# A hybrid RG-LRU and gated-delta-rule block: the order of all instructions planned anew, with a clock in the planner and a table of shifts to its priorities

## The chip, the cores and the metric

The kernel runs on one core of a Trainium2 chip. The core has a matrix engine (TensorE, PE in the profile; its weight loads are the row PEld), a vector engine (VectorE, DVE), a scalar engine (ScalarE, ACT), GpSimd (POOL) and a sync engine (SyncE, SP), which here issues every DMA. Each engine works through its own instructions in the order in which the program holds them; semaphores hold an instruction back until what it needs is there. The metric is the device time of one execution in microseconds (us): the median of the runs shown.

## The reference, cut to what matters

One layer on 1024 tokens of width 1024, all in float32:

```python
mod = silu(c) @ w_mod + b_mod                     # six vectors: sh1, sc1, g1, sh2, sc2, g2
h = rms_norm(x, norm_mix_w) * (1 + sc1) + sh1
proj = h @ w_in                                   # (1024, 3080): x_lru, y_lru, q, k, v, z, beta, alpha
xr = causal_conv(x_lru) + bias                    # RG-LRU half: two gates, a scan over the tokens,
out_lru = rms_norm(rg_lru(xr, ...) * gelu(y_lru)) # times gelu(y)
q, k, v = silu(causal_conv(q, k, v))              # gated delta rule half: 4 heads of 128
o = gated_delta_rule_chunked(q, k, v, g, beta)    # per chunk a triangular solve, then a recurrence
out_gdn = rms_norm(o) * silu(z)
x = x + g1 * (concat(out_lru, out_gdn) @ w_out)
h = rms_norm(x, norm_mlp_w) * (1 + sc2) + sh2
x = x + g2 * (square(relu(h @ w_up)) @ w_down)    # width 4096
out = rms_norm(x, final_norm_w)
```

## The kernel before

Nothing is issued where it is written. The body calls proxies (`PE`, `V`, `A`, `G`, `SP` for the five engines), and `Recorder.add` stores each call as an `Op` with an estimated duration (`Proxy.length`) and its dependencies. At the end `schedule` simulates the engines with these durations and picks one order for each engine; `emit` issues in that order. All instructions therefore carry one source line, that of the helper (L328 before the change, L427 after it), and the profile is read by names of tiles.

What sets the order: the big products form the *backbone* (`bb`): the projections in the sequence k0, k1, k2, k3, z0 to z3, q0, v0, q1, v1 and so on, then lx and ly (the two RG-LRU inputs), `wg` and `wl` (the output projection, GDN and LRU half), the MLP `up` and `dn`. They run in that fixed sequence. Everything else is side work: it has a latest start `lst`, from which a priority `pri` is made, and side work that is ready goes ahead of the backbone. The backbone is thus the filler in which side work on TensorE (token transposes, small products) finds its place.

Names that the steps below need. A projection is done in thirds of 342 tokens, `k0_p2`, `k0_p0`, `k0_p1`, 24 matmuls each (three products of a high and a low half of the operands: `hh`, `hl` and `_wh`, `_wl`). `sh1_c` turns the summed shift vector `sh1_acc` into columns; the third that ends the tokens needs it, as does `ab2`, the last third of beta and alpha. For head h, `key` makes `k{h}T` (a convolution of four VectorE or ScalarE steps, then a silu whose tanh is `k{h}th`), its transposes `ktok{h}`, the Gram products `kk{h}`, norms `ssk`, `rnk`, coefficients `bcoef`, the decay matrix `k{h}_dm` (GpSimd adds a mask `neg` to the broadcast `k{h}_gb`, ScalarE takes exp, GpSimd multiplies by `bcoef`) and the chunk matrix `LT`. `inverse` needs all four heads: a forward substitution of 31 steps on VectorE (`ftmp`, `xx`), transposes `xnc` and `xtc`, 16 copies into `xn` on ScalarE, and four rounds of small products on TensorE, `ie`, `ig`, `ih`, `ix`. `chain` is the recurrence over 8 chunks for each head: `ch` (three products a step), `r` and the state `S` on VectorE, `vn` on ScalarE, `cho` the output. `gate` are the gate products of RG-LRU, from `xrh` and `xrl`. `h2T` are the transposes ahead of the MLP. `z_wl`, `q_wl`, `v_wl` are low halves of weights, made by GpSimd.

Of the kernel before, what the change touches and what calls it, by code (L numbers as in the profile page):

```python
# [3 lines left out]

# [7 lines left out]
F32R = mybir.dt.float32r  # L12
AF = mybir.ActivationFunctionType
# [26 lines left out]
LAT = {("PE", "DVE"): 0.2, ("PE", "ACT"): 0.2, ("ACT", "DVE"): 0.04, ("DVE", "ACT"): 0.04, ("ACT", "POOL"): 0.08,  # L40
       ("DVE", "POOL"): 0.08, ("POOL", "DVE"): 0.04, ("POOL", "ACT"): 0.04, ("DVE", "PE"): 0.06, ("ACT", "PE"): 0.06,
       ("POOL", "PE"): 0.06, ("DVE", "DVE"): 0.04, ("ACT", "ACT"): 0.04, ("POOL", "POOL"): 0.05, ("PE", "PE"): 0.0}
COLD = 11.0
SC1_SUM = 5
SIDE_SCALE = 1.4
TINY_RUN, TINY_SHARE = 0.2, 1.0
# [1 line left out]
LOAD_WINDOW, DUE = 40.0, 5.0  # L48
# [3 lines left out]
class Buf:  # L52


    def __init__(self, pool, tag, bufs, shape, dt, name, proto):
        self.pool, self.tag, self.bufs, self.shape, self.dt, self.name, self.proto = pool, tag, bufs, shape, dt, name, proto
        self.tile = None
        self.key = (id(pool), tag)
        self.left = 0
        self.last = 0.0  # L60
        self.held = False
        self.pri = 1e9

    def get(self):
        if self.tile is None:
# [52 lines left out]
    return ap.name, (0, 1, lo, lo + sum((n - 1) * st for st, n in ap.ap) + 1)  # L118


class Op:
    __slots__ = ("port", "eng", "fn", "a", "k", "outs", "ins", "dur", "bb", "preds", "succs", "allocs", "bufs", "lst", "ready",
                 "need", "load", "bias", "pri", "tiny")


class Recorder:
# [11 lines left out]
    def add(self, eng, fn, a, k, outs, ins, dur, port=False):  # L138
        op = Op()
        op.port = port  # L140
        op.eng, op.fn, op.a, op.k, op.dur, op.bb, op.load = eng, fn, a, k, dur, self.bb and eng == "PE", False
        op.bias = None if self.early else self.bias
        op.tiny = self.tiny
        op.preds, op.succs, op.allocs = {}, [], []
        i = len(self.ops)
        op.bufs = {}
        for is_out, aps in ((False, ins), (True, outs)):
            for ap in aps:
                key, box = ap.box() if isinstance(ap, View) else dram_box(ap)
# [12 lines left out]
        if op.bb:
# [12 lines left out]
    def schedule(self):  # L175
        ops = self.ops
# [5 lines left out]
        for i in range(len(ops) - 1, -1, -1):  # L182
            op = ops[i]
            t = op.lst if op.bb else t
            op.pri = i - 1e5 if op.bias is None else op.lst if op.bb else min(op.lst, t + DUE + op.bias) + 1e-6 * i
        order = []
        now = {e: 0.0 for e in ("PE", "DVE", "ACT", "POOL", "SP")}
        dma = tend = 0.0
# [21 lines left out]
        while done < len(ops):  # L210
# [21 lines left out]
            i = heapq.heappop(avail[e])[1]  # L232
            if e == "PE" and debt > TINY_RUN:

                j = next((j for j in avail[e] if ops[j[1]].bb), None)
                if j:
                    avail[e].remove(j)
                    heapq.heapify(avail[e])
                    heapq.heappush(avail[e], (cls(ops[i]), i))
                    i = j[1]  # L240
            op = ops[i]
            t = now[e]
            wait = None
            while bbn < len(bbq) and ops[bbq[bbn]].ready is None:
                bbn += 1
            ref = ops[bbq[bbn]].lst if bbn < len(bbq) else 0.0
            op.allocs = [b for b in op.bufs if b.held != "in"]
            for b in op.allocs:
                f = free[b.key]
                q = queue[b.key]  # L250
                while q and q[0].held == "in":
                    q.pop(0)
                keep = 0
                lim = RESERVE.get(b.tag, 0)
                for o in q:
                    if o.pri >= op.pri or keep >= lim and (o.pri > -5e4 or o.tag != "b"):
                        break
                    if o.held != "in" and o is not b:
                        keep += 1
                if (op.load or not op.preds) and op.pri - ref > LOAD_WINDOW:  # L260
                    wait = ("t", t + 1.0)
                elif len(f) <= keep:
                    wait = ("b", b.key)
                elif f[0][0] > t + 1e-6:
                    wait = ("t", f[0][0])
                if wait:
                    break
# [11 lines left out]
            if e == "SP":  # L279
                now[e] = t + 0.05  # L280
                dma = max(dma, t + 1.25) + op.dur
                fin = dma
            else:
                t = max(t, port) if op.port else t
                now[e] = fin = t + op.dur * (2 if e == "PE" and t < COLD else 1)
                port = max(port, fin) if op.port else port
            op.ready = None
            order.append(i)
            done += 1
            for b in op.bufs:  # L290
                b.left -= 1
                b.last = max(b.last, fin)
# [38 lines left out]
def free_size(ap):  # L331
    n = 1
    for d in ap.shape[1:]:
        n *= d
    return n


class Proxy:
# [26 lines left out]

    def length(self, name, out, ins, k):
        n = max([free_size(out)] + [free_size(v) for v in ins[:1]])
        ptr = sum(free_size(v) == 1 for v in ins[1:]) and n > 1
# [7 lines left out]
        if self.eng == "DVE":  # L376
# [1204 lines left out]
```

## Time and profile before

| | |
|---|---|
| median of 3 runs | 1186.23 us (1186.09 to 1186.87) |
| the profiled execution | 1185.62 us, of which 1183.8 us lie between its first and last instruction (the span) |
| busy in the span | PE 1145.0, PEld 984.2, DVE 828.9, ACT 616.8, POOL 373.5 us |
| mean granted TensorE clock | 0.989 |
| 16 DMA engines | 55.9% busy with the kernel's own queue, 229.52 MB moved |

The profile is one execution. A row of its timeline gives the start (us from the first instruction), the length, the engine, the operation with its output and inputs, how many were merged, and in brackets how long the engine stood idle before and what released it. A busy engine is not always an engine at full rate: PE rows overlap, since matmuls are pipelined. The clock of TensorE falls to half in some stretches; the views by window give its mean.

### The profile page before, as it was taken

How to read it: one execution, taken by the hardware profiler on the slowest of the kernel's cores; microseconds unless marked ns; L12 is line 12 of the kernel's file. 1: busy time of each engine (PE TensorE's matmuls, PEld its weight loads, DVE VectorE, ACT ScalarE, POOL GpSimd, SP SyncE). 2: the span in 40 equal slices, each digit the busy share in tenths (PEclk: the TensorE clock that was granted, in tenths of full speed). 3: DMA queues.
4: the chain of work that ended last, by engine and by line, in shares of the span. 5: the costliest groups of instructions: out<-in, count | busy, mean ns of one | idle time of the engine just before them, and what ended most of it. 6: DMA issues, size and time to landing. Idle time of an engine off the chain costs nothing.

```text
span 1183.8 us, 15997 instructions
## 1 busy us (share of the span) xinstructions
PE 1145.0 (97%) x5952; PEld 984.2 (83%) x5952; DVE 828.9 (70%) x1123; ACT 616.8 (52%) x988; POOL 373.5 (32%) x221
## 2 busy tenths in 40 slices
PE   6799899999999999999999999999999999999997
PEld 3699899999999998877888888888788888888885
DVE  5757696578887798977966666756767556785553
ACT  5537327445455868277655555555555533353441
POOL 1319611345323472410011212121430075732130
PEclk9899899999999999999999999999999999999999
DMA  9703432533553525323077778776899767865631
GB/s 323 240 21 142 143 107 78 182 116 108 181 192 90 196 86 217 107 107 116 32 237 257 244 262 251 258 237 231 314 405 402 273 213 251 298 234 186 205 143 71
DMA packets 127151, 229.52 MB, mean 194 GB/s; under 512 B 10657, under 2 KB 51806, under 8 KB 127074
## 3 DMA queue, kind: packets, MB, share of 16 engines
q1 hardware_dynamic: 127074, 228.51, 55.9%
q8 instruction: 46, 0.75, 0.3%
q14 instruction: 31, 0.25, 0.1%
HBM read 171.83 MB, written 56.65 MB: 193 GB/s over the span
## 4 chain that ended last, share of the span: by engine, by line
PE 82%; DVE 8%; DMA 3%; ACT 3%; issue 2%; POOL 1%; SPq 1%; POOLq 0%; DVEq 0%; ACTq 0%
PE dn L328 26%; PE upx L328 15%; PE upz L328 8%; PE upy L328 4%; PE v_p L328 3%; PE q_p L328 3%; PE ly_p L328 3%; PE wg L328 3%; PE wl L328 3%; PE z_p L328 2%; PE k_p L328 2%; PE lx_p L328 2%; PE ch L328 2%; DVE xr L328 1%; SPq L328 1%
## 5 line engine op out<-in xcount | busy, mean ns | idle before, releaser
L328 PE MATMUL upx<-h2h,U 128*128 128x512 f32 x512 | 167.8, 394 | 0.0
L328 POOL TENSOR_TENSOR wd<-wd,wd 128x512 f32<-128x512 f32 x32 | 44.5, 1397 | 233.2 <-DMA wd<-in_w_down_dram 186.6
L328 PEld LDWEIGHTS upx<-h2h,U 128*128 128x128 f32 x512 | 96.1, 188 | 22.7
L328 PE MATMUL upx<-h2l,U 128*128 128x512 f32 x256 | 101.0, 395 | 0.0
L328 ACT ACTIVATE act<-act 128x512 f32<-128x512 f32 x112 | 70.9, 633 | 57.7 <-DVE act L328 55.5
L328 DVE TENSOR_TENSOR U<-wu,U 128x512 fp32r<-128x512 f32 x112 | 79.9, 733 | 18.0 <-ACT U L328 18.0
L328 PE MATMUL upz<-h2h,U 128*128 128x512 f32 x256 | 85.0, 394 | 0.0
L328 ACT CAST U<-wu 128x512 fp32r<-128x512 f32 x112 | 66.7, 617 | 14.1 <-PE upz L328 4.9
L328 DVE TENSOR_TENSOR act<-upz,ek 128x512 f32<-128x512 f32 x32 | 22.1, 691 | 56.5 <-PE upz L328 39.8
L328 PEld LDWEIGHTS upz<-h2h,U 128*128 128x128 f32 x256 | 48.1, 188 | 11.4
L328 PEld LDWEIGHTS upx<-h2l,U 128*128 128x128 f32 x256 | 48.1, 188 | 11.4
L328 ACT COPY ek<-upx 128x512 f32<-128x512 f32 x48 | 28.1, 585 | 48.2 <-PE upx L328 48.0
L328 PE MATMUL upz<-h2l,U 128*128 128x512 f32 x128 | 50.4, 394 | 0.0
L328 POOL TENSOR_TENSOR xb<-xb,keep 128x512 f32<-128x512 f32 x8 | 12.5, 1562 | 120.2 <-DVE keep L328 120.2
L328 PE MATMUL upy<-h2h,U 128*128 128x512 f32 x128 | 42.7, 394 | 0.0
L328 ACT ACTIVATE vn<-ch,bcoef 128x128 f32<-128x128 f32 x32 | 11.8, 368 | 53.0 <-PE ch L328 52.9
L328 POOL TENSOR_TENSOR ssq<-ssq,mhalf 128x1 f32<-128x1 f32 x16 | 11.3, 706 | 89.0 <-DVE ssq L328 88.9
L328 PE MATMUL k_p<-hl,k_wh 128*128 128x342 f32 x96 | 32.8, 341 | 0.3 <-DVE hl L328 0.3
L328 PE MATMUL k_p<-hh,k_wh 128*128 128x342 f32 x96 | 32.5, 339 | 0.4 <-ACT hh L328 0.4
L328 DVE TENSOR_TENSOR wu<-wu,wu 128x512 f32<-128x512 f32 x48 | 32.5, 682 | 0.2 <-DMA wu<-in_w_up_dram 0.2
L328 PE MATMUL k_p<-hh,k_wl 128*128 128x342 f32 x96 | 32.3, 336 | 0.0
L328 PE MATMUL v_p<-hh,v_wl 128*128 128x342 f32 x96 | 32.1, 335 | 0.0
(574 smaller groups left out, 3733.6 us busy)
## 6 DMA issues: line engine op xcount, KB each, us to landing
L<-aod SPq DMA_DIRECT2D x56, 512.0 KB, 7.0
R<-in_w_down_dram SPq DMA_DIRECT2D x40, 512.0 KB, 5.6
wu<-in_w_up_dram SPq DMA_DIRECT2D x32, 512.0 KB, 4.3
aod<-as SPq DMA_DIRECT2D x64, 256.0 KB, 2.4
wd<-in_w_down_dram SPq DMA_DIRECT2D x32, 512.0 KB, 4.8
aod<-act SPq DMA_DIRECT2D x48, 256.0 KB, 2.1
x<-in_x_dram SPq DMA_DIRECT2D x16, 512.0 KB, 4.8
sc_w<-in_w_mod_dram SPq DMA_DIRECT2D x16, 512.0 KB, 6.3
```

The lines of the kernel that those rows point to most:

```text
L328: op.fn(*[res(v) for v in op.a], **{n: res(v) for n, v in op.k.items()})
```

## The change

The planner is altered, and with it the order on every engine; what is computed, by which instructions and on which engine, stays as it was.

[...]
- A table `SHIFTS`, found by a search, holds one number for each of the 8378 recorded operations (2910 are not zero); a quarter of it, in us, is added to the priority of side work. Backbone operations and those recorded as `early` (the first loads and their use) take no shift.
- An accumulation that starts a PSUM tile anew must follow the one that ended in it; loads that are held back for being over 40 us ahead of the backbone are woken when the backbone has moved on, and no longer tried again each us; after small side work the backbone operation that comes next is the lowest in priority, and no longer the first found; durations with two column operands get two additions.

The core of the diff:

```diff
+_SHIFTS = (
+    'c-qaId2m(NeaC<AJ?ZI5LLdnV0RkZwiG4R<wm^)7YrMprIwncm)J@}Qn;B2s&a}-;-8P+MlCeAWA6YtW)=nmlGmY(z3C0fC21AT77@NiHn8ip4f%'
...
+SHIFTS = array.array("h", zlib.decompress(base64.b85decode(_SHIFTS))) if _SHIFTS else None
+class Clock:
+    def __init__(self):
+        self.end, self.work, self.over, self.half = HAM_0, 0.0, 0.0, True
+
+    def run(self, t, dur, work):
+        while t >= self.end:
+            share = self.work / HAM_W
+            self.half = share < HAM_UP if self.half else share < HAM_DOWN
+            self.end += HAM_W
+            self.work = min(self.over, HAM_W)
+            self.over -= self.work
+        if self.half:
+            dur, work = 2.0 * dur, 2.0 * work
+        now = min(work, self.end - t)
+        self.work += now
+        self.over = work - now
+        return dur
...
+        op.adj = SHIFTS[len(self.ops)] / 4.0 if SHIFTS else 0.0
+        op.work = min(dur, (1 if ins[-1].dtype == F32R else 2 if fn.__name__ == "transpose" else 4)
+                      * free_size(outs[0]) / 2400.0) if eng == "PE" else 0.0
...
-            op.pri = i - 1e5 if op.bias is None else op.lst if op.bb else min(op.lst, t + DUE + op.bias) + 1e-6 * i
+            op.pri = i - 1e5 if op.bias is None else op.lst if op.bb else min(op.lst, t + DUE + op.bias) + op.adj + 1e-6 * i
...
-                j = next((j for j in avail[e] if ops[j[1]].bb), None)
+                j = min((j for j in avail[e] if ops[j[1]].bb), default=None)
...
-                    wait = ("t", t + 1.0)
+                    wait = ("l", 0)
...
-                now[e] = fin = t + op.dur * (2 if e == "PE" and t < COLD else 1)
+                now[e] = fin = t + (clock.run(t, op.dur, op.work) if e == "PE" else op.dur)
...
-            return (0.145 if psum else 0.155) + n / (1920.0 if fast else 960.0) + (0.06 if ptr else 0.0)
+            return (0.145 if psum else 0.155) + n / (1920.0 if fast else 960.0) + 0.06 * ptr
```

Three places show what moved. The numbers behind the names only tell buffers apart.

GpSimd, where the decay matrices of the four key heads are made. Before:

```order
L328 TENSOR_TENSOR rnk_943<-ssk_921,mhalf_115 128x8
L328 TENSOR_TENSOR k0_dm_972<-k0_gb_905,neg_140 128x1024
L328 TENSOR_TENSOR k1_dm_1015<-k1_gb_908,neg_140 128x1024
L328 TENSOR_TENSOR k2_dm_1041<-k2_gb_929,neg_140 128x1024
L328 TENSOR_TENSOR k3_dm_1060<-k3_gb_974,neg_140 128x1024
L328 TENSOR_TENSOR k0_dm_972<-k0_dm_972,bcoef_987 128x1024
L328 MEMSET xt0_1083 128x1024
```

The same place on GpSimd after the change:

```order
L427 TENSOR_TENSOR k0_dm_935<-k0_gb_894,neg_120 128x1024
L427 TENSOR_TENSOR k1_dm_961<-k1_gb_896,neg_120 128x1024
L427 TENSOR_TENSOR k2_dm_1004<-k2_gb_963,neg_120 128x1024
L427 TENSOR_TENSOR k3_dm_1030<-k3_gb_968,neg_120 128x1024
L427 TENSOR_TENSOR rnk_1046<-ssk_937,mhalf_104 128x8
L427 MEMSET xn0_1060 128x1024
L427 TENSOR_TENSOR k0_dm_935<-k0_dm_935,bcoef_1063 128x1024
```

The norm of head 0 (`rnk`), which waits for VectorE, stood ahead of the four mask additions, and now stands behind them.

VectorE, about the convolution of the third key head, `k2T`. Before:

```order
L328 TENSOR_TENSOR LT_1085<-kk0_0_912,k0_dm_972 128x512
L328 TENSOR_TENSOR LT_1085<-kk0_1_923,k0_dm_972 128x512
L328 SCALAR_TENSOR_TENSOR k2T_984<-k2_st_366,cols_485,k2T_984 128x1024
L328 TENSOR_TENSOR bcoef_987<-beta_727,rnk_943 128x8
L328 SCALAR_TENSOR_TENSOR ncoef_1019<-ssk_921,rnk_943 128x8
L328 TENSOR_TENSOR bcoef_987<-bcoef_987,rnk_943 128x8
L328 SCALAR_TENSOR_TENSOR k2T_984<-k2_st_366,cols_485,k2T_984 128x1024
L328 COPY k3_b_1150<-k3_p2_948 128x1
L328 SCALAR_TENSOR_TENSOR k2T_984<-k2_st_366,cols_485,k2T_984 128x1024
L328 TENSOR_TENSOR LT_1085<-kk1_0_1005,k1_dm_1015 128x512
L328 TENSOR_TENSOR LT_1085<-kk1_1_1012,k1_dm_1015 128x512
L328 SCALAR_TENSOR_TENSOR k2T_984<-k2th_1187,k2T_984 128x1024
```

The same place on VectorE after the change; the first of the three steps of `k2T` stands seven instructions ahead of the first row here:

```order
L427 TENSOR_TENSOR bcoef_1063<-beta_735,rnk_1046 128x8
L427 SCALAR_TENSOR_TENSOR ncoef_1065<-ssk_937,rnk_1046 128x8
L427 TENSOR_TENSOR bcoef_1063<-bcoef_1063,rnk_1046 128x8
L427 SCALAR_TENSOR_TENSOR k2T_959<-k2_st_337,cols_475,k2T_959 128x1024
L427 COPY k3_b_1080<-k3_p2_951 128x1
L427 SCALAR_TENSOR_TENSOR k2T_959<-k2_st_337,cols_475,k2T_959 128x1024
L427 TENSOR_TENSOR LT_1114<-kk0_1_930,k0_dm_935 128x512
L427 TENSOR_TENSOR LT_1114<-kk0_0_918,k0_dm_935 128x512
L427 SCALAR_TENSOR_TENSOR k2T_959<-k2th_1116,k2T_959 128x1024
```

The convolution of `k2T` stood behind the `LT` rows of head 0 and its end behind those of head 1; now its three steps stand ahead of the former and its end ahead of the latter. On TensorE `ktok2` and `kk2`, which use it, stand 11 matmuls into `z0`, where they stood 54 matmuls into it; `ktok3` and `kk3` stand where they stood, two matmuls into `z1`.

TensorE, about the shift vector in the opening. Before:

```order
L328 MATMUL k1_p1_578<-hh3_300,k1_wh_423 128x342
L328 MATMUL k1_p1_578<-hl3_317,k1_wh_423 128x342
L328 MATMUL sh1_c_595<-ones_104,sh1_acc_445 128x1 x8
L328 MATMUL k1_p1_578<-hh3_300,k1_wl_436 128x342
L328 MATMUL k1_p1_578<-hh4_371,k1_wh_423 128x342
```

The same place on TensorE after the change:

```order
L427 MATMUL k1_p1_573<-hh7_388,k1_wh_427 128x342
L427 MATMUL k1_p1_573<-hl7_395,k1_wh_427 128x342
L427 MATMUL sh1_c_608<-ones_132,sh1_acc_409 128x1 x8
L427 MATMUL k1_p1_573<-hh7_388,k1_wl_442 128x342
L427 MATMUL ab2_639<-hh0_278,wab1_314 16x342
```

Twelve of the 13 matmuls of `k1_p1` that stood between `sh1_c` and `ab2` now stand ahead of `sh1_c`. Farther on, 14 matmuls of `v0_p2` stand ahead of the first `ie`, where 4 stood, and the first `ie` is that of head 3, behind six of the `xn` copies on ScalarE, where it was head 0's behind four; `gate20` and `gate2512` begin 10 matmuls into `ly3_p1`, where they began ahead of `ly3_p2`, 58 backbone matmuls earlier; the `h2T` of six of the eight token tiles stand 1 to 4 matmuls later, of one 8 earlier. The small vectors `alog` and `dtb` are loaded after `k3_w` and no longer ahead of `sh1_w`. On TensorE the order from the last `h2T` to the end is the same but for the place of four small products for `g2`; on the other engines it differs to nearly the end.

More of the change, by code (lines that the diff above doesn't have):

```diff
@@ L1 @@
+import array
+import base64
 import heapq
 import math
+import zlib
 from contextlib import ExitStack
@@ L42 @@
        ("POOL", "PE"): 0.06, ("DVE", "DVE"): 0.04, ("ACT", "ACT"): 0.04, ("POOL", "POOL"): 0.05, ("PE", "PE"): 0.0}
-COLD = 11.0
+HAM_W, HAM_0, HAM_DOWN, HAM_UP = 3.4133, 0.5, 0.5, 0.75
 SC1_SUM = 5
@@ L62, in __init__ @@
         self.pri = 1e9
+        self.sum = None
     def get(self):
@@ L121 @@
 class Op:
-    __slots__ = ("port", "eng", "fn", "a", "k", "outs", "ins", "dur", "bb", "preds", "succs", "allocs", "bufs", "lst", "ready",
+    __slots__ = ("adj", "work", "port", "eng", "fn", "a", "k", "outs", "ins", "dur", "bb", "preds", "succs", "allocs", "bufs", "lst", "ready",
                  "need", "load", "bias", "pri", "tiny")
@@ L161, in add @@
                 (ws if is_out else rs).append((box, i))
+        if eng == "PE" and fn.__name__ == "matmul":
+            b = outs[0].buf
+            if k["start"] and b.sum is not None:
+                op.preds.setdefault(b.sum, 0)
+            elif not k["start"] and k["stop"]:
+                b.sum = i
         if op.bb:
@@ L193, in schedule @@
         bbn = tmp = 0
+        ref, late = ops[bbq[0]].lst, []
         port = 0.0
+        clock = Clock()
         debt = 0.0
@@ L243, in schedule @@
             wait = None
-            while bbn < len(bbq) and ops[bbq[bbn]].ready is None:
-                bbn += 1
-            ref = ops[bbq[bbn]].lst if bbn < len(bbq) else 0.0
             op.allocs = [b for b in op.bufs if b.held != "in"]
@@ L270, in schedule @@
                     heapq.heappush(fut[e], (wait[1], i))
+                elif wait[0] == "l":
+                    heapq.heappush(late, (op.pri, i))
                 else:
@@ L289, in schedule @@
             done += 1
+            if op.bb:
+                bbn += 1
+                ref = ops[bbq[bbn]].lst if bbn < len(bbq) else 0.0
+                while late and late[0][0] - ref <= LOAD_WINDOW:
+                    j = heapq.heappop(late)[1]
+                    heapq.heappush(fut[ops[j].eng], (max(ops[j].ready, t), j))
             for b in op.bufs:
@@ L367, in length @@
         n = max([free_size(out)] + [free_size(v) for v in ins[:1]])
-        ptr = sum(free_size(v) == 1 for v in ins[1:]) and n > 1
+        ptr = sum(free_size(v) == 1 for v in ins[1:]) if n > 1 else 0
         psum = any(isinstance(v, View) and v.buf.tag == "ps" for v in ins)
@@ L381, in length @@
                 return 0.05 + n / 550.0
-            return (0.145 if psum else 0.155) + n / (1920.0 if fast else 960.0) + (0.06 if ptr else 0.0)
+            return (0.145 if psum else 0.155) + n / (1920.0 if fast else 960.0) + 0.06 * ptr
         if self.eng == "ACT":
-            return (0.16 if psum else 0.195) + n / 1200.0 + (0.1 if ptr or "accum_out" in k else 0.0)
+            return (0.16 if psum else 0.195) + n / 1200.0 + 0.1 * max(ptr, "accum_out" in k)
         if k.get("op") == ALU.pow:
```

49 lines of the change are left out of this document (added).

## The prediction

> **What bounds the kernel now.** First the page's head and its chain of work that ended last, then TensorE's idle time by stage.
>
> ```profile
> span 1183.8 us, 15997 instructions
> PE 82%; DVE 8%; DMA 3%; ACT 3%; issue 2%; POOL 1%; SPq 1%; POOLq 0%; DVEq 0%; ACTq 0%
> ```
>
> TensorE carries 82% of the chain. So the question is where it is not running. The next view gives the busy time of each engine in stretches that I cut at the stages (columns: stretch, its length, PE, PEld, DVE, ACT, POOL, granted clock, DMA share, GB/s).
>
> ```profile
> 0.00:60.00 60.00, 43.85 (x219) 30.04 (x220) 39.63 (x75) 31.80 (x49) 16.24 (x22) 0.91 0.82 278
> 60.00:113.00 53.00, 53.00 (x348) 50.98 (x348) 33.61 (x87) 30.50 (x75) 25.82 (x18) 0.97 0.20 81
> 113.00:135.00 22.00, 16.75 (x103) 16.21 (x102) 15.83 (x27) 10.38 (x19) 17.71 (x17) 0.84 0.46 161
> 172.00:210.00 38.00, 36.37 (x313) 36.02 (x312) 28.42 (x46) 25.73 (x50) 6.88 (x4) 1.00 0.28 89
> 210.00:310.00 100.00, 100.00 (x705) 99.47 (x705) 74.00 (x100) 46.78 (x81) 38.92 (x15) 1.00 0.46 151
> 310.00:345.00 35.00, 32.62 (x234) 31.68 (x233) 30.61 (x39) 16.68 (x29) 16.40 (x7) 1.00 0.35 108
> 345.00:400.00 55.00, 53.38 (x360) 51.53 (x358) 42.95 (x54) 35.96 (x53) 18.71 (x7) 1.00 0.44 142
> 400.00:500.00 100.00, 98.45 (x521) 87.48 (x520) 90.02 (x74) 61.27 (x78) 49.30 (x20) 1.00 0.44 158
> 500.00:557.00 57.00, 54.44 (x265) 43.62 (x263) 40.27 (x92) 39.46 (x83) 5.16 (x8) 1.00 0.32 111
> 557.00:1176.00 619.00, 619.00 (x2670) 500.21 (x2668) 400.74 (x465) 307.06 (x453) 168.56 (x99) 1.00 0.69 238
> 1176.00:1183.80 7.80, 0.17 (x1) 0.00 (x0) 2.29 (x4) 1.44 (x3) 0.55 (x1) 0.63 0.26 98
> ```
>
> Length less PE is what an order can win. From 557 to 1176 it is zero: 619 us that no order shortens. The opening idles 16.2 us under a DMA share of 0.82, the end 7.6 us behind the last matmul; both are mostly chains that the change leaves in place. What remains is 5.25 us at the key heads (113 to 135), 1.6 at the triangular inverse (172 to 210), and 2.4 + 1.6 + 1.55 + 2.6 = 8.1 us in recurrence, gates and second norm. Third view: what TensorE waited for there (us in total, times, longest).
>
> ```profile
> PE ktok L328 <- DVE k3T L328: 4.2, 1, 4.2
> PE sh_c L328 <- DVE hab L328: 2.1, 1, 2.1
> PE ch L328 <- DVE r L328: 1.7, 2, 1.3
> PE ie L328 <- ACT xn L328: 1.6, 1, 1.6
> PE gate L328 <- ACT xrh L328: 1.6, 2, 1.4
> PE ch L328 <- DVE S L328: 1.5, 2, 1.2
> PE h2T L328 <- DVE h2r L328: 1.5, 3, 0.5
> PE ktok L328 <- DVE k2T L328: 1.1, 1, 1.1
> ```
>
> Fourth, the clock, by windows of the trace's own stretches (same columns):
>
> ```profile
> 61.95:65.36 3.41, 3.41 (x14) 2.85 (x13) 1.54 (x15) 1.46 (x7) 1.88 (x1) 0.50 0.00 0
> 113.16:116.57 3.41, 2.33 (x21) 2.07 (x20) 3.23 (x5) 2.97 (x7) 3.27 (x6) 1.00 0.39 156
> 116.57:119.99 3.42, 3.42 (x26) 3.42 (x25) 3.42 (x7) 0.78 (x1) 2.80 (x3) 1.00 0.28 109
> 123.40:130.20 6.80, 5.53 (x26) 5.56 (x27) 5.06 (x8) 3.86 (x8) 4.68 (x7) 0.50 0.35 143
> ```
>
> After the wait for `k3T` TensorE ran 5.5 us at half clock, which costs 5.5 / 2 = 2.8 us more. After `sh_c` one stretch of 3.4 us cost 1.7.
>
> **The change part by part.** No instruction is added or removed, so each term is a wait that goes, comes or moves.
>
> *Opening.* Twelve matmuls now run ahead of `sh1_c`, and four more of `k1_p0` stand between `rows_ps` and it. A matmul of 342 columns lasts 26.29 / 166 = 0.158 us by this row of the chain:
>
> ```profile
> 130.02 26.29 PE z_p L328 x166
> ```
>
> Twelve are 1.9 us of work in a wait of 2.1 us. But `ab2` now follows `sh1_c` at once and must wait for `sh1`, which the 13 matmuls covered; I estimate 0.7 us for two small steps between (0.36 each, like `bcoef` below), and 0.6 us more idle ahead of `rows_ps`, whose cover loses the four matmuls (4 x 0.158). Gain 2.1 - 0.7 - 0.6 = 0.8 us; bounds 2.1 (the whole wait) and -1.3 (the wait stays, the new one comes). The SP queue loses two small loads ahead of `sh1_w`, worth at most their issue; taken as nothing, because the DMA engines are at 0.82.
>
> *Key heads.* GpSimd, VectorE and one row of TensorE, by the timeline (the last bracket is the idle time ahead of the row):
>
> ```profile
> 90.15 2.61 POOL L328 TENSOR_TENSOR rnk<-ssk,mhalf 128x8 f32<-128x8 f32 x1 [23.39 <-DVE ssk L328]
> 92.73 10.21 POOL L328 TENSOR_TENSOR k_dm<-k_gb,neg 128x1024 f32<-128x1024 f32 x4
> 104.83 1.29 DVE L328 TENSOR_TENSOR LT<-kk,k_dm 128x512 f32<-128x512 f32 x2 [4.15 <-POOL k_dm L328]
> 113.23 1.21 DVE L328 SCALAR_TENSOR_TENSOR k2T<-k2th,k2T 128x1024 f32<-128x1024 f32 x1
> 114.50 1.09 PE L328 MATMUL ktok<-ident,k2T 128*128 128x128 f32 x8 [1.07 <-DVE k2T L328]
> 122.00 2.52 DVE L328 SCALAR_TENSOR_TENSOR k3T<-k3th,k3T 128x1024 f32<-128x1024 f32 x1 [0.54 <-ACT k3th L328]
> 133.73 0.36 DVE L328 TENSOR_TENSOR bcoef<-beta,rnk 128x8 f32<-128x8 f32 x1
> ```
>
> GpSimd stood 23 us until `ssk` let `rnk` go, though the masks behind it need only their loads. VectorE then stood 4.15 us before `LT`, with all of `k2T` queued behind. In the new order the four masks go first, `LT` of head 0 can start about when it did (104 to 105), but three steps of `k2T` are done by then: its last step starts near 104.9 and ends near 106, 8 us sooner than 114.4. From there to the end of `k3T` stand four steps of 1.2 us, four `ktail` and `ssk` rows, two `LT` and the copies that `k3th` now waits for, by estimate 12 us in all: 118, where it was 124.5. TensorE, which stood at `ktok2` from 114.5 - 1.07 = 113.4, reaches it 43 matmuls sooner and the opening's 0.8 sooner, at 113.4 - 43 x 0.158 - 0.8 = 105.8, waits 0.3, does `ktok2` and `kk2` (3.6 us: 1.09 for eight transposes, about 2.5 for the products) and 63 matmuls (10 us) and is at `ktok3` at 119.7. So the waits of 4.2 and 1.1 shrink to 0.3, and with them the half clock.
>
> *What is late next.* Not all of that is kept, since the inverse hangs on the same chain. `bcoef` of head 3 was at 133.7; now it stands behind the end of `z1_p2` (119.7 + 3.6 + 22 x 0.158 = 126.8), then `ssk` and `rnk` (1.6 to 2.6): 129. The first `ie` started at 177.43 after a wait of 1.63:
>
> ```profile
> 177.43 0.94 PE L328 MATMUL ie<-xn,LT 128*128 128x128 f32 x6 [1.63 <-ACT xn L328]
> ```
>
> From `bcoef` to it are 177.4 - 133.7 = 43.7 us, so `ie` can start at 172.7, 4.7 sooner. TensorE is there at about 169 (177.4 - 1.6 = 175.8 before, less 5.0 of the waits at `ktok2` and `ktok3`, less 2.8 of clock, less 0.8 of the opening, plus 1.6 for the ten matmuls of `v0`: 168.8), and waits some 3 to 4 us. The ten matmuls are 1.6 us done ahead of it; two more `xn` copies ahead of the first `ie` cost 0.8 by their row:
>
> ```profile
> 175.73 6.65 ACT L328 COPY xn<-xnc 32x256 f32<-32x256 f32 x16 [3.74 <-DVE xnc L328]
> ```
>
> Opening, key heads and inverse together: 4.7 + 1.6 - 0.8 = 5.5 us. The chain of 43.7 us is itself uncertain. GpSimd and VectorE held each other up in it:
>
> ```profile
> 171.04 2.39 POOL L328 TENSOR_TENSOR q_dm<-q_gb,neg 128x1024 f32<-128x1024 f32 x1 [18.32 <-DMA q_gb<-gdr]
> 171.05 2.43 DVE L328 TENSOR_TENSOR xx<-xx,ftmp 128x31 f32<-128x31 f32 x1
> ```
>
> A step whose neighbours take 0.2 took 2.4. One such meeting more or less is 2.2 us; so 5.5 lies between 1 (two more) and 12 (nothing of any wait is left: 2.1 + 5.25 + 1.6 + 2.8).
>
> *Recurrence, gates, second norm.* These hold 8.1 us of idle. `gate20` waited 1.4 for `xrh`; ahead of it now stand 58 more matmuls, 9 us, and that wait goes. The `h2T` moved by one to four matmuls of 0.23 us each (619 / 2670) cover waits of 0.4 to 0.7. The two waits for `S` and `r` have one cause:
>
> ```profile
> 330.67 1.28 DVE L328 SCALAR_TENSOR_TENSOR v3T<-v_st,cols,v3T 128x1024 f32<-128x1024 f32 x1 [0.45 <-ACT v3T L328]
> 331.99 3.28 DVE L328 SCALAR_TENSOR_TENSOR v3T<-v_st,cols,v3T 128x1024 f32<-128x1024 f32 x1
> 335.79 0.33 DVE L328 SCALAR_TENSOR_TENSOR S<-S,egl,ch 128x128 f32<-128x128 f32 x1
> ```
>
> The step of `v3T` ahead of `S` took 3.28 us, the same step just before it 1.28; `S` was late and TensorE stood for the next `ch`. Which steps meet GpSimd so in the new order the order does not say. I take two thirds of the 8.1 as gone, 5.4 us, because about that much of it has a mover I can name (`gate` 1.6, `h2T` 1.5, `ch` 1.7 + 1.5, an estimate of one third left over); bounds 0 and 8.1.
>
> *New stalls.* From 210 to 310 TensorE idles not at all today, yet there too the hand-offs `ch`, `r`, `S`, `vn` stand in a new order. A meeting such as that of 331.99 costs TensorE about the longest wait for `S`, 1.2 us. I charge one of them, 1.0 us; bounds 0 and 4 (three or four).
>
> *At no cost.* After 557 the orders of VectorE, ScalarE, GpSimd and SP differ nearly to the end, TensorE's does not. What hides that is 619 us of products without a gap; with VectorE busy 401 of them and the DMA engines at 0.69 there is room. If a transfer of weights came late, all of the lateness would show; nothing in the trace of before is late there, so it is taken at nothing. The extra dependence in PSUM and the changed durations live in the planner alone.
>
> *Sum.* 5.5 + 5.4 - 1.0 = 9.9 us off the profiled execution's 1185.6 (span 1183.8, 1.8 around it): 1175.7. The median of the runs stands 0.6 above that execution, so 1176.3; I say 1176.0.
>
> [...] In the window 113.16 to 116.57 TensorE was busy 2.33 of 3.41 us, the eight transposes `ktok2` among it, and the next stretch ran at 1.00. [...]
>
> **The rivals.**
>
> B, *the gain of the key heads turns up as a wait at `ie`.* For it: the 43.7 us from `bcoef` to `ie` hold a chain on VectorE that the order interleaves anew, and TensorE already waited 1.6 there. If two more steps of 2.4 us fall into it, `ie` starts at 177.5 as now, and of the 5.5 only the 0.8 of matmuls done ahead less copies stays. Against it: steps of VectorE in that chain met GpSimd before too, so the 43.7 already hold such meetings. Then the gain is 0.8 + 5.4 - 1.0 = 5.2: 1181.0.
>
> C, *nearly all waits go.* 5.25 + 1.6 + 8.1 of idle, 2.8 + 1.7 of clock at the two waits, less the 0.3 left over at `ktok2`: 19.2, so 1167. For it: each wait has work beside it that can be put ahead. Against it: the same VectorE must serve all of them, and it is busy 90 of 100 us from 400 to 500.
>
> D, *slower: the recurrence hangs on steps that GpSimd holds up.* 32 steps of a head and chunk, each with three hand-offs between TensorE and another engine, are 96 places. Where a 128x1024 step of VectorE stands ahead of `r` or `S` and meets GpSimd, TensorE loses 1.2 us. From (9.9 + 1.0 + 2.4) / 1.2 = 11 of them on the kernel is slower; at 13 it stands at 1185.6 - 10.9 + 15.6 = 1190.3, some 1190. For it: 74 of 100 us of VectorE and 39 of GpSimd are full in 210 to 310. Against it: only two such waits exist today in as dense a traffic.
>
> E, *the change does nothing*: the waits end where they end because of durations that the planner does not know, and new ones take their places. Then 1186. For it: the wait of 4.2 for `k3T` is one that a planner with true durations would hardly have left.
>
> [...]
>
> **How the numbers follow.** A, the sum, 0.62 (1170 to 1180.5); B 0.15; C 0.08; D 0.07; E 0.05; F 0.03. The forecast is that of A. The range takes in A, B, F and half of C: 1168 to 1183, with D, E and the rest of C outside, 0.16 to 0.2. A difference under 0.2% (2.4 us) can't be told from none with this kernel. A, B, C and F end beyond it on the fast side but for the slow edge of B: faster 0.87; E and that edge are same, 0.06; D slower, 0.07.
>
> **What the profile after would show.** Right: the wait of TensorE for `k3T` under 1 us and for `sh1_c` under 1; granted clock 1.00 in the windows about `z0` and `z1`; VectorE not waiting 4 us for `k_dm`; the first `ie` at about 173, still behind a wait of 2 to 4 us; no wait at `gate` for `xrh`; the products from the last `h2T` to the end as long as now. Wrong: idle time between 210 and 310, or half clock there; `ie` as late as 177; or waits of `ch` for `r` and `S` above 5 us in all, which would be D.

## The result, and the profile after

The changed kernel takes 1164.55 us (median of 4 runs, 1164.21 to 1167.03), the kernel before 1186.16 us beside it: a ratio of 0.9825, interval 0.9807 to 0.9843, so 1.6 to 1.9% faster. The profiled execution took 1164.43 us, its span is 1162.6. The direction was right and the size wrong: 1164.55 lies below the range of 1168 to 1183 and far from the forecast of 1176. Rival C, "nearly all waits go" (1167, given 0.08), came nearest.

First the page's head and the chain of waits after the change.

```profile
span 1162.6 us, 15986 instructions
PE 91%; DMA 3%; DVE 3%; ACT 1%; issue 1%; SPq 1%; POOL 0%; POOLq 0%; ACTq 0%
```

TensorE carries 91% of the chain, where it was 82%; VectorE fell from 8% to 3%. Next the same stretches of time by window (columns as before). The new order runs 4 to 21 us ahead of the old one there, so a window no longer holds quite the same work.

```profile
0.00:60.00 60.00, 45.82 (x241) 32.52 (x241) 38.76 (x81) 31.89 (x49) 14.48 (x20) 0.97 0.82 278
60.00:113.00 53.00, 51.85 (x351) 49.59 (x352) 42.61 (x90) 33.44 (x82) 31.34 (x25) 1.00 0.29 100
113.00:135.00 22.00, 22.00 (x149) 21.98 (x149) 14.97 (x30) 11.16 (x21) 15.69 (x17) 1.00 0.44 143
172.00:210.00 38.00, 38.00 (x312) 38.00 (x311) 20.54 (x29) 21.87 (x39) 14.67 (x6) 1.00 0.30 94
210.00:310.00 100.00, 99.09 (x705) 97.61 (x704) 82.41 (x111) 49.32 (x86) 32.60 (x13) 1.00 0.49 159
310.00:345.00 35.00, 35.00 (x256) 34.98 (x255) 30.86 (x42) 17.57 (x31) 13.91 (x6) 1.00 0.55 181
345.00:400.00 55.00, 54.53 (x362) 53.18 (x361) 40.42 (x45) 42.00 (x55) 22.84 (x9) 1.00 0.43 134
400.00:500.00 100.00, 100.00 (x501) 86.14 (x500) 83.93 (x92) 58.82 (x84) 41.25 (x19) 1.00 0.44 153
500.00:557.00 57.00, 55.88 (x267) 45.57 (x265) 47.18 (x91) 42.62 (x84) 2.94 (x5) 1.00 0.22 79
```

The idle time in the window of the key heads (5.25 us) is 0, of the inverse (1.6) 0, and of recurrence, gates and second norm (8.1) 2.5, of which 0.9 is new between 210 and 310. The key heads still wait once, 0.9 us at `ktok2`, which now falls into 60 to 113. What TensorE still waits for beyond the opening:

```profile
PE rows_ps L427 <- DMA rows<-in_gdn_norm_w_dram: 2.4, 1, 2.4
PE h2T L427 <- DVE h2r L427: 1.1, 2, 0.6
PE ktok L427 <- DVE k2T L427: 0.9, 1, 0.9
PE ch L427 <- DVE r L427: 0.7, 1, 0.7
PE gate L427 <- ACT xrh L427: 0.5, 1, 0.5
```

(The first row is the opening's.) The waits for `k3T`, `hab`, `xn` and `S` are gone. The clock of TensorE, too, is better: the trace of before has four stretches of half clock between 12 us and the last product, 20.5 us in all, two beside those at 61.95 and 123.40 that the prediction shows:

```profile
20.98:24.39 3.41, 3.41 (x5) 0.44 (x4) 2.63 (x7) 3.07 (x5) 0.00 (x0) 0.50 1.14 280
41.46:48.28 6.82, 5.06 (x20) 4.97 (x21) 3.45 (x6) 1.64 (x2) 0.58 (x1) 0.50 0.74 196
```

In the profiled execution after the change a single one is left:

```profile
42.88:46.30 3.42, 3.42 (x15) 3.36 (x14) 3.42 (x5) 1.22 (x2) 0.09 (x1) 0.50 0.93 232
```

Where the 21.2 us between the two spans went can be counted. I call *lost time* the time from the first matmul up to a point, less the work done till then, each matmul taken at the median spacing of its kind where nothing waits (by both traces 0.157 us for 342 columns, 0.232 for 512, 0.109 for a transpose). The work is the same in both, 1124.9 us.

| up to | lost before | lost after | gained in the stretch |
|---|---|---|---|
| end of `ab2` (67.2 / 63.2 us) | 27.2 | 23.2 | 4.0 |
| end of `z3` (163.6 / 152.4) | 36.4 | 25.2 | 7.2 |
| end of `v0` (219.4 / 206.2) | 38.4 | 25.1 | 2.1 |
| end of `v3` | 39.2 | 26.3 | -0.4 |
| end of `ly` | 46.4 | 28.1 | 5.4 |
| end of `wl` | 49.9 | 29.0 | 2.6 |
| last `dn` | 50.9 | 29.7 | 0.3 |

### The profile page after: what moved, and what is told of

Read it like the earlier page. It is cut to its first block, busy times and chain, and to the rows that moved or that the text cites. A ratio compares the mean times of both kernels' runs of the same rounds, so it can differ in the third digit from the quotient of the medians.

```text
span 1162.6 us, 15986 instructions
## 1 busy us (share of the span) xinstructions
PE 1137.1 (98%) x5952; PEld 979.8 (84%) x5952; DVE 834.6 (72%) x1123; ACT 616.5 (53%) x988; POOL 371.4 (32%) x221
## 4 chain that ended last, share of the span: by engine, by line
PE 91%; DMA 3%; DVE 3%; ACT 1%; issue 1%; SPq 1%; POOL 0%; POOLq 0%; ACTq 0%
PE dn L427 26%; PE upx L427 15%; PE upz L427 8%; PE wg L427 4%; PE upy L427 4%; PE wl L427 4%; PE z_p L427 4%; PE lx_p L427 4%; PE q_p L427 4%; PE ly_p L427 4%; PE v_p L427 3%; PE k_p L427 2%; PE ch L427 2%; SPq L427 1%; DMA sh_w<-in_w_mod_dram 1%
## 5 line engine op out<-in xcount | busy, mean ns | idle before, releaser
L427 POOL TENSOR_TENSOR wd<-wd,wd 128x512 f32<-128x512 f32 x32 | 49.9, 1568 | 214.4 <-DMA wd<-in_w_down_dram 163.4
L427 DVE TENSOR_TENSOR U<-wu,U 128x512 fp32r<-128x512 f32 x112 | 85.0, 774 | 18.1 <-ACT U L427 17.9
L427 POOL TENSOR_TENSOR R<-R,R_5o 128x1024 f32<-128x1024 f32 x8 | 20.0, 2520 | 74.4 <-DMA R<-in_w_down_dram 63.2
L427 DVE TENSOR_TENSOR wu<-wu,wu 128x512 f32<-128x512 f32 x48 | 36.1, 759 | 0.5 <-DMA wu<-in_w_up_dram 0.4
L427 PE MATMUL ly_p<-hh,ly_wh 128*128 128x342 f32 x96 | 31.7, 330 | 0.0
```

Of the source, the lines that this page charges most:

```text
L427: op.fn(*[res(v) for v in op.a], **{n: res(v) for n, v in op.k.items()})
```

## The experiments

Two theories stood at the start. One: the gain is a sum over stretches of time, each of which gives what its lost time says. The other, rival B of the prediction: much of it is lost again at the next hand-off. Beside that, who carries it: the planner's new rules or the table; and within the key heads, which of the moves that the prediction named.

**Planner and table apart.**

```diff
 planner_alone (new planner)
-SHIFTS = array.array("h", zlib.decompress(base64.b85decode(_SHIFTS))) if _SHIFTS else None
+SHIFTS = None
 table_alone (planner of before)
+        op.adj = SHIFTS[len(self.ops)] / 4.0
-            ... min(op.lst, t + DUE + op.bias) + 1e-6 * i
+            ... min(op.lst, t + DUE + op.bias) + op.adj + 1e-6 * i
```

> The new planner with its table taken out (SHIFTS = None). Theory 'the table carries the gain': the clock model alone reorders much and gains little, 1178 to 1187 us; GpSimd's four masks stand in two pairs around rnk here, so TensorE still waits 2 us or more for k2T or k3T. Rival 'the clock model carries it': 1165 to 1171.

> The planner of before with the table added to its priorities (and the rule that a new accumulation follows the one that ended in its PSUM tile). Theory 'the table carries the gain': a few side steps move whatever the clock model, 1165 to 1176 us. Rival 'the table only works with the planner that it was searched with': 1182 or more, with new waits of TensorE.

Measured: planner_alone 1188.71 us, ratio 1.0025 (1.0007 to 1.0043); table_alone 1203.97, 1.0152 (1.0137 to 1.0167). Neither gains; only both together do. Planner_alone, just above its range of 1178 to 1187, still waits for `k3T`, and table_alone found a new wait, with half clock behind it (waits of each kernel, then a window of table_alone):

```profile
PE sh_c L376 <- DVE hab L376: 4.4, 1, 4.4
PE ktok L376 <- DVE k3T L376: 3.2, 1, 3.2
```

```profile
PE gate L393 <- ACT xrh L393: 17.9, 2, 16.3
```

```profile
458.65:475.72 17.07, 3.08 (x7) 2.48 (x8) 17.07 (x14) 8.00 (x10) 8.12 (x3) 0.50 0.17 61
```

The numbers are differences against one planner's priorities; against another's they put `gate` where its input is 16.3 us away. The theory "the table carries the gain" holds for planner_alone, in that the planner's new rules, its class `Clock` among them, gain nothing without it, and fails for table_alone, whose rival was right.

**Stretches of time.** Here the orders of all five engines are spliced: what the one order has issued up to a point is kept, the rest follows in the other.

```diff
-        for i in self.schedule():
+        for i in ORDER:   # first_part: the new order to the end of z3, then the old; second_part: the reverse;
+                            # opening_new, opening_old: the same two, spliced at the end of ab2; window_new: old, new, old
```

> The new order on all engines up to the end of z3 (152 us), the old order beyond. Theory 'gains of the stages add': by the two traces 11.2 us of lost TensorE time go up to there, 1186.2 - 11.2 = 1175.0, and up to 2.4 us come back as a wait at ie, since TensorE then arrives 11.2 us sooner and the inverse only 8.8: 1175 to 1177.5. Rival B of the prediction (the gain is lost at ie): 1181 or more.

> The old order up to the end of z3 (163.5 us), the new order beyond. Theory 'gains of the stages add': 21.2 - 11.2 = 10.0 us go in ie, recurrence, gates and second norm, 1176.2 us (1175 to 1178). Rival: the new order beyond depends on the early one, since its hand-offs are fitted to when the heads are ready: 1180 or more.

> The new order on all engines up to the end of ab2 (63 us), the old order beyond. Theory 'stretches add': 4.0 us of lost TensorE time go up to there by the two traces, 1186.2 - 4.0 = 1182 us (1181 to 1183.5). Rival 'the opening carries the key heads': the decay chain gT, k_gb, masks comes 4 us sooner with it, so the wait for k3T shrinks too: 1179 or less. Rival 'given back': 1185 or more.

> The old order up to the end of ab2 (67 us), the new order beyond. Theory 'stretches add': 21.2 - 4.0 = 17.2 us go: 1169 us (1167.5 to 1170.5). Rival 'the opening carries the key heads': without it the masks start 4 to 5 us later, k2T and k3T with them, and the waits come back: 1173 or more.

> The old order up to the end of ab2, the new order on all five engines up to the end of z3, the old order beyond. Theory 'an order is fitted on all engines of a stretch, and stretches add': opening_old less second_part is 6.7 us, first_part less opening_new 6.4: 1186.2 - 6.5 = 1179.7 us (1178.5 to 1181). Rival: the stretch gains only with the new opening or the new inverse at its ends: 1183 or more.

| new order in | median, us | ratio (interval) | lost time promised |
|---|---|---|---|
| opening to `ab2` (opening_new) | 1180.86 | 0.9958 (0.9943 to 0.9973) | -4.0 us, 0.9966 |
| `ab2` to `z3` (window_new) | 1178.32 | 0.9948 (0.9934 to 0.9962) | -7.2, 0.9939 |
| opening to `z3` (first_part) | 1174.48 | 0.9907 (0.9892 to 0.9922) | -11.2, 0.9906 |
| `z3` to the end (second_part) | 1176.81 | 0.9925 (0.9908 to 0.9942) | -10.0, 0.9916 |
| `ab2` to the end (opening_old) | 1170.12 | 0.9865 (0.9851 to 0.9878) | -17.2, 0.9855 |

Stretches add. The ratios of opening, window and second_part make 5.0 + 6.2 + 8.9 = 20.1 us of the 20.8 that 0.9825 stands for, and each interval holds what the lost time promised. Three of the five medians lie a little below the range expected for them (first_part, opening_new and window_new, by 0.1 to 0.5 us). Nothing comes back at `ie` (rival B falls), and the opening's 4 us do not shrink the waits at the key heads: in opening_new the wait for `k3T` is 4.2 us as before, since VectorE and TensorE both come 4 us sooner (`LT` of head 0 starts at 100.94, where it started at 104.83):

```profile
100.94 1.29 DVE L554 TENSOR_TENSOR LT<-kk,k_dm 128x512 f32<-128x512 f32 x2 [1.86 <-POOL k_dm L554]
```

In window_new, with the old opening and the old rest, the key heads wait only this long:

```profile
PE ktok L554 <- DVE k2T L554: 0.7, 1, 0.7
```

**Single engines in the key heads.** The edits move rows of one or two engines and leave all other orders as they were.

```diff
 masks_first, GpSimd of before (masks_early: also issued right behind the loads k_gb)
-rnk<-ssk  k0_dm  k1_dm  k2_dm  k3_dm
+k0_dm  k1_dm  k2_dm  k3_dm  rnk<-ssk
 k2T_ahead, VectorE of before
-LT LT k2T bcoef ncoef bcoef k2T k3_b k2T LT LT k2T(end)
+k2T k2T k3_b k2T LT LT k2T(end) bcoef ncoef bcoef LT LT
 both_moves: the two together
 vector_scalar: k2T_ahead, and on ScalarE of before
-gc x4 ... k2th
+k2th gc x4 ...
 rnk_first, GpSimd of after: rnk back ahead of the masks
 k2T_behind, VectorE of after: the three steps of k2T back behind LT of head 0
```

> The order of before with one instruction moved: on GpSimd rnk of head 0 stands behind the four mask additions. Theory M (LT of head 0 waits for GpSimd's masks, and all that is queued behind it on VectorE comes as much sooner): LT starts near 101 instead of 104.8, k3T and bcoef of head 3 end 3.5 to 4.5 us sooner, the wait for k3T falls from 4.2 to under 1, and the first ie comes 3.5 to 4.5 sooner: 1182 to 1183.5 us. Theory V (the prediction's: what counts is the place of k2T on VectorE, LT starts when it did): 1186 within 1.

> The order of before, on VectorE the three steps of k2T moved ahead of LT of head 0 and its end ahead of LT of head 1. Theory V: k3T ends near 118 instead of 124.5, the waits for k2T and k3T go, ie starts near 173: 1181.5 us. Theory M: LT of head 1 still waits for GpSimd until 112, k3T behind it ends near 122.5, gain about 2: 1184.

> The order of before with both moves, of rnk on GpSimd and of k2T on VectorE. Theory M with V: k3T ends near 116 as in the new order, no wait for it, no half clock at 123 to 130; of the 8 us that this frees at z1 the inverse lets 6 to 8 through: 1178 to 1180.5 us. Rival B of the prediction: the wait at ie takes the most, 1183 or more.

> The new order with one instruction moved back: on GpSimd rnk of head 0 ahead of the four mask additions. Theory M: the masks end 10 us behind ssk, LT of head 0 starts 5.4 later (106.6), TensorE waits 5 us more at ktok2 and gets a half-clock stretch of 1.7 to 3.4: 1169.5 to 1173 us. Theory V: k2T's steps stand ahead of LT, so little is lost, 1164.5 to 1166.

> The order of before; on GpSimd the four mask additions right behind their loads (their buffers taken there too, so that they no longer wait for one that ssk frees), rnk of head 0 behind them. Theory M: masks from 85, LT of head 0 near 101 instead of 104.8, k3T 3 to 4 us sooner: 1182.5 to 1184.5 us. Rival 'an order is fitted on all five engines at once': rnk and bcoef come 3 to 4 us later, VectorE waits there with all its queue, and the old places on ScalarE and TensorE don't fit: 1186 or more.

> The order of before; the steps of k2T ahead of LT on VectorE as in k2T_ahead, and k2th on ScalarE ahead of the four copies gc of head 0, which wait for LT. Theory 'a place on one engine needs the others': k2th no longer waits for LT (114.5 in k2T_ahead), k2T ends near 111, k3T near 121; total 1182.5 to 1185.5 us, 6 or more below k2T_ahead. Rival 'k2T's place is worth nothing, since its steps beside the masks take twice as long': 1187 or more.

> The new order; on VectorE the three steps of k2T behind LT of head 0, where the old order had them. Theory V: LT starts near 100, k2T ends near 107.4 instead of 103.5, the wait at ktok2 grows from 0.9 to near 4.8, and a stretch of half clock may follow: 1168.5 to 1171 us. Rival 'k2T's place is worth nothing': 1164 to 1166.

| kernel | median, us | ratio to before (interval) |
|---|---|---|
| masks_first | 1189.85 | 1.0024 (1.0015 to 1.0032) |
| masks_early | 1189.61 | 1.0028 (1.0015 to 1.0041) |
| k2T_ahead | 1192.05 | 1.0040 (1.0028 to 1.0053) |
| both_moves | 1194.02 | 1.0058 (1.0046 to 1.0071) |
| vector_scalar | 1187.51 | 1.0008 (0.9997 to 1.0020) |
| rnk_first | 1173.34 | 0.9889 (0.9873 to 0.9904) |
| k2T_behind | 1169.74 | 0.9860 (0.9845 to 0.9876) |

Put into the old order, neither move that the prediction named gains, alone, together or with `k2th`; vector_scalar can't be told from before, the others are 0.2 to 0.6% slower. Taken out of the new order, each costs: k2T_behind 5.6 us against after_again, rnk_first 7.6 by the ratios. The time of k2T_behind fell where its theory V had it, that of masks_early where its rival had it. In masks_first and k2T_ahead both theories missed; both_moves lies in the range of its rival (1183 or more), but with other waits than the rival's, 3.7 us at `k1T` and 6.7 at `k3T`; rnk_first came 0.3 above theory M's range, with `LT` of head 0 at 107.87 (106.6 expected).

In masks_first the masks started when `rnk` had (90.30 and 90.15), 2.4 us sooner than before. They now ran beside two steps of `k1T` on VectorE, which took 3.50 and 2.18 us instead of 1.28 and 1.23, and `rnk` came only at 101.62, so that VectorE waited for it. `LT` of head 0 started at 106.50, and no sooner than before (timeline of GpSimd and VectorE, then a wait of TensorE, which is new):

```profile
90.30 11.37 POOL L509 TENSOR_TENSOR k_dm<-k_gb,neg 128x1024 f32<-128x1024 f32 x4 [22.41 <-DVE ssk L509]
92.64 3.50 DVE L509 SCALAR_TENSOR_TENSOR k1T<-k_st,cols,k1T 128x1024 f32<-128x1024 f32 x1
```

```profile
PE ktok L509 <- DVE k1T L509: 3.7, 1, 3.7
```

In k2T_ahead VectorE did the steps of `k2T` sooner, but two of them ran beside GpSimd's last mask addition and its product with `bcoef` and took 6.27 us; and the end of `k2T` waits for `k2th`, which ScalarE's unchanged order held behind copies `gc` that wait for `LT` (timeline of VectorE and ScalarE):

```profile
100.88 6.27 DVE L509 SCALAR_TENSOR_TENSOR k2T<-k_st,cols,k2T 128x1024 f32<-128x1024 f32 x2
109.70 1.69 ACT L509 COPY gc<-LT 32x256 f32<-32x256 f32 x4 [4.19 <-DVE LT L509]
114.50 1.04 ACT L509 ACTIVATE k2th<-k2T 128x1024 f32<-128x1024 f32 x1
115.57 1.23 DVE L509 SCALAR_TENSOR_TENSOR k2T<-k2th,k2T 128x1024 f32<-128x1024 f32 x1 [5.91 <-ACT k2th L509]
```

With `k2th` moved too (vector_scalar) `k2T` is done at 112.2 instead of 116.8, and 3.8 us of the time are back by the ratios (1.0040 to 1.0008), but no gain is left: `k3T` still stands behind `LT` of head 1, which waits for GpSimd, and TensorE waits for it longer than before.

```profile
116.07 1.29 DVE L509 TENSOR_TENSOR LT<-kk,k_dm 128x512 f32<-128x512 f32 x2 [3.61 <-POOL k_dm L509]
```

```profile
PE ktok L509 <- DVE k3T L509: 6.7, 1, 6.7
```

So vector_scalar missed its expected 1182.5 to 1185.5, and its rival (1187 or more) gave the time, though not by the mechanism alone that it named: k2T_behind shows that the place is worth 5.6 us against after_again (1169.74 to 1164.17) where the other engines fit it. k2T_behind itself went as expected, a wait of 4.4 and half clock behind it (a wait, then a window):

```profile
PE ktok L554 <- DVE k2T L554: 4.4, 1, 4.4
```

```profile
106.16:112.98 6.82, 4.43 (x21) 4.43 (x22) 4.07 (x9) 5.46 (x10) 4.96 (x8) 0.50 0.28 111
```

What held the masks in masks_first and masks_early is not settled: they began 5.0 us behind the first issue of `k_gb` in both (85.3 and 84.7), 4.4 in the new order, which fits the load; the profile names `ssk`, whose rows differ between the two runs by the same 0.6 us.

**The waits that are left.** Five, then four of them, were filled by moving steps of TensorE behind backbone products.

```diff
 trimmed4, TensorE of after
-ktok2 kk2 | q3_p1 x3, ch1_3 | gate10 | h2T5_0 h2T5_0 ...
+z0 x7, ktok2 kk2 | ch1_3 5 products later | gate group 4 later | two pairs of h2T 3 later
 trimmed: the same, and rows_ps 17 products later, cols on VectorE behind four hl
```

> The new order with five waits of TensorE filled by hand: rows_ps 17 products later (the copy cols on VectorE behind four hl), ktok2 and kk2 7 later, one ch 5 later, one group of gate 4 later, two pairs of h2T 3 later. Theory 'what is left are places too': 2.4 + 0.9 + 0.7 + 0.5 + 1.1 = 5.6 us of waits go, and 1.7 of half clock behind rows_ps with them: 1157.5 to 1160.5 us. Rival: ready times behind them bind (hl, hh, LT), the waits move on: 1163 to 1166.

> The new order with four waits of TensorE filled by hand (ktok2 and kk2 7 products later, one ch 5, one group of gate 4, two pairs of h2T 3), the opening left as it is. Theory 'what is left are places': 0.9 + 0.7 + 0.5 + 1.1 = 3.2 us less than the new order, 1161 to 1162 us. Rival: the waits move on to the next step, within 1 us of the new order.

> The new order itself, given as a list: 1164.5 us (1164 to 1167), to compare trimmed4 with on the same chip.

Measured: trimmed 1163.41 (ratio 0.9809, 0.9794 to 0.9824), which can't be told from the new order. On one chip, trimmed4 1162.00 (1161.49 to 1163.32; ratio 0.9796, 0.9782 to 0.9811) and after_again 1164.17 (1163.89 to 1167.21; 0.9822, 0.9805 to 0.9838): trimmed4 is 2.2 us faster where 3.2 were expected. All its runs lie below all of after_again's, though the two intervals overlap. It is the fastest kernel of this study. Of the waits, `gate` stayed at 0.5 and 0.3 came new:

```profile
PE gate L554 <- ACT xrh L554: 0.5, 1, 0.5
PE cho L554 <- ACT vn L554: 0.3, 1, 0.3
```

The time of trimmed is in its rival's range (1163 to 1166). In its trace the wait at `rows_ps` (2.4) went, and the waits for `hh` grew from 1.0 to 2.2 us. Whether that is the rival's "ready times bind" is not shown: this execution has three stretches of half clock in the opening where the one of the new order has one, and first_part, with the same three and the opening unchanged, waits 2.0 us for `hh` as well.

```profile
PE k_p L554 <- ACT hh L554: 2.2, 3, 1.0
```

## Why the prediction was wrong, and where it was right

The span fell by 21.2 us where the sum had 9.9. Of the 11.3 that it was short, the opening makes 3.2, key heads and inverse 4.6, and the rest of the kernel 3.6 (rounded). The three steps that failed are the opening's price, the 43.7 us from `bcoef` to `ie` taken as fixed, and idle time taken as the upper bound.

*Opening: forecast 0.8, measured 4.0 of lost time and 5.0 by opening_new.* The failing step is the size of the term. I charged 0.7 for `ab2` and 0.6 for `rows_ps`; neither came (`ab2` waited 0.2, and the wait at `rows_ps` fell from 3.7 to 2.4). And I left the clock out of it: of half clock I had named the 1.7 us behind `sh_c` and not counted them, and the stretches at 20.98 and 41.46 I had not looked for. Between 12 us and `ab2` the trace of before has 13.65 us at half clock, the one after 3.41. How much of that belongs to the order and how much to the execution is not separated: the trace of first_part has the new opening with 10.2 us at half clock and loses 3.1 us more in it than the trace after.

*Key heads: right.* `LT` of head 0 was to "start about when it did"; in the new order it started at 101.18, 3.65 sooner. That is the opening's gain seen again: opening_new, with the old order of the key heads, has it at 100.94. Window_new has the old opening and the new key heads, and there `LT` started at 104.63 (forecast 104 to 105), `k2T` ended at 107.1 (106), `k3T` at 119.0 (118), and `bcoef` of head 3 stood at 128.33 (129). Up to `ab2` that execution, the fastest of its five, lost 0.3 us less than the trace of before, so nothing of the opening is in these times. Timeline of window_new, then of after, in the order of the rows of before:

```profile
104.63 1.28 DVE L554 TENSOR_TENSOR LT<-kk,k_dm 128x512 f32<-128x512 f32 x2
105.83 1.23 DVE L554 SCALAR_TENSOR_TENSOR k2T<-k2th,k2T 128x1024 f32<-128x1024 f32 x1
117.75 1.23 DVE L554 SCALAR_TENSOR_TENSOR k3T<-k3th,k3T 128x1024 f32<-128x1024 f32 x1 [1.45 <-ACT k3th L554]
128.33 0.17 DVE L554 TENSOR_TENSOR bcoef<-beta,rnk 128x8 f32<-128x8 f32 x1 [1.75 <-POOL rnk L554]
```

```profile
83.37 8.08 POOL L427 TENSOR_TENSOR k_dm<-k_gb,neg 128x1024 f32<-128x1024 f32 x3 [13.75 <-DMA k_gb<-gdr]
101.18 1.27 DVE L427 TENSOR_TENSOR LT<-kk,k_dm 128x512 f32<-128x512 f32 x2
102.39 1.23 DVE L427 SCALAR_TENSOR_TENSOR k2T<-k2th,k2T 128x1024 f32<-128x1024 f32 x1
114.31 1.23 DVE L427 SCALAR_TENSOR_TENSOR k3T<-k3th,k3T 128x1024 f32<-128x1024 f32 x1 [1.45 <-ACT k3th L427]
124.89 0.17 DVE L427 TENSOR_TENSOR bcoef<-beta,rnk 128x8 f32<-128x8 f32 x1 [1.75 <-POOL rnk L427]
166.00 1.95 PE L427 MATMUL ie<-xn,LT 128*128 128x128 f32 x16
```

One reading in it was wrong without harm to the sum. I had read the 23 us of GpSimd as a wait that `rnk` caused; masks_first showed that moving `rnk` alone starts the masks only 2.4 us sooner. In the new order they start at 83.37, since the loads `k_gb` come 5.4 us sooner as well (79.0 for 84.4), most of it by the opening. The waits fell to 0.9 (0.3 forecast), and the half clock of 123 to 130 went, as forecast.

*Inverse: forecast `ie` at 172.7 behind a wait of 3 to 4, measured 166.0 with none.* TensorE was forecast there at 168.8; with the opening's 3.2 us it came when it should. The step that failed is the chain from `bcoef` of head 3, which I carried over with its 43.7 us. Up to the first `xn` copy that chain took 175.73 - 133.73 = 42.0 us before and 162.35 - 124.89 = 37.5 after (37.4 in window_new), so the copies no longer held `ie` up. VectorE's wait for `gc` in it, which ScalarE issues behind a `z_st` that waits for TensorE, fell by 1.8 us, and one meeting with GpSimd less (two steps of 2.4 us or more, three before) makes 2.2 (VectorE of before, VectorE of after, ScalarE of after):

```profile
140.53 2.11 DVE L328 STREAM_TRANSPOSE gg<-gc 128x1024 f32<-128x1024 f32 x1 [3.66 <-ACT gc L328]
129.69 2.12 DVE L427 STREAM_TRANSPOSE gg<-gc 128x1024 f32<-128x1024 f32 x1 [1.84 <-ACT gc L427]
162.35 4.16 ACT L427 COPY xn<-xnc 32x256 f32<-32x256 f32 x10 [1.56 <-DVE xnc L427]
```

So opening, key heads and inverse gave 13.3 instead of 5.5, above my bound of 12, which held neither the opening's clock nor more than one of its waits.

*Recurrence, gates, second norm: forecast 5.4 less 1.0, measured 8.0 (21.2 - 13.3).* The new stall came about as charged: 0.9 us idle between 210 and 310. The step that failed is the bound: I took the idle time of 8.1 as the most that could go, and the lost time there was 50.9 - 38.4 = 12.5. Each wait costs more than the idle that a window shows, since in both traces the row of a matmul of 342 columns is 0.32 us long while the next starts after 0.157: the busy time hides the tail. At `ie` before, the row's idle was 1.63 and the extra spacing 1.79; the waits at `h2T` show 0.5 and cost 0.67. The 15 waits behind `v0` in the trace of before, 8.1 of idle, cost 10.7 of spacing so; what makes up the rest to 12.5 is not shown.

*Of the rivals:* B, D and E fell; C had the mechanism, and its price of 1167 was short by the same undercount. F, which has 0.03 of the chances, stands for half clock behind `ktok2` and `ktok3`; no run shows that term. In the trace after, the window at `ktok2` held 0.94 us of idle and most of eight transposes, and the next ran at full clock (two windows of after); behind `ktok3`, from 116.57 to 123.40, the clock stayed at 1.00 too.

```profile
100.91:104.32 3.41, 2.47 (x18) 2.20 (x17) 2.98 (x7) 2.83 (x6) 3.30 (x4) 1.00 0.00 0
104.32:107.74 3.42, 3.42 (x30) 3.42 (x28) 2.75 (x5) 2.39 (x4) 3.25 (x5) 1.00 0.67 265
```

As forecast, the new order did not change the time from the last `h2T` to the last product: 1175.78 - 556.97 = 618.8 before, 1154.57 - 536.25 = 618.3 after.

What stood against rival C, and so behind its 0.08, was that one VectorE could not serve all waits at once. It could: it was busy 828.9 us before and 834.6 after, in the same span less 21 us.

## What to carry to other kernels

Count what a new order can win as lost time (span less work at unhindered spacing), stretch by stretch, and not as idle time: here it was 12.5 us where the windows showed 8.1, and the stretches' gains added when spliced together. When a later stage starts sooner than forecast, ask first whether an earlier stage handed the time down, before its own step is called wrong; an order spliced at the seam of the two answers that. Do not judge a reordering, or port it, by single moves on one engine: no move that looked like the cause gained in the old order, and each taken out of the new order cost 5.6 to 7.6 us; the traces show queues of other engines (`rnk` on GpSimd, `k2th` on ScalarE) that held the moved steps up. Numbers found for one planner made the other slower here (1.0152), and a few of the waits that are left could still be filled by hand (2.2 us here).

## What the hardware showed that was not expected

The half-clock stretches do not fall at the same places in each execution of one order. first_part has the opening of the new order word for word, yet its profiled execution had three such stretches, at other places than the one at 42.88, and took 1176.23 us where its other runs took 1174.35 to 1174.59.

```profile
32.01:35.42 3.41, 3.41 (x17) 3.18 (x15) 2.11 (x5) 3.41 (x5) 0.55 (x1) 0.50 1.02 412
62.73:66.14 3.41, 3.41 (x14) 1.71 (x14) 1.42 (x13) 0.23 (x3) 0.00 (x0) 0.50 0.00 0
```

Within a trace the starts of such stretches lie whole multiples of 3.41 us apart, the length of the shortest: 32.01, 52.49 and 62.73 in first_part (6 and 3 times 3.41), 20.98, 41.46, 61.95 and 123.40 in before (6, 6 and 18 times). From one trace to the other they do not: the 42.88 of after lies 10.87 us, 3.2 times 3.41, behind the 32.01 of first_part, whose opening is the same. A planner that fixes the time at which its first window ends, as `Clock` does, can thus be right for some executions only. Whether its rule for the next window is the chip's was not tested.

Two VectorE steps of 1.28 us took 6.27 us beside a mask addition of GpSimd and a product of 2.88 us (k2T_ahead): 3.1 each, 1.9 more than the third step of `k2T` in the same run (1.28), which is most of a mask addition (10.21 / 4 = 2.55). A move of VectorE work into a stretch that GpSimd fills should be priced by such a row.
